# An expert-choice router on rows not yet normed: tile 6's and half of tile 7's routing inside the last output projection

## The chip, the cores and the metric

The kernel runs on one core of one Trainium2 chip. The metric is the device time of one execution in microseconds (us), as the median of several. The engines are TensorE (PE; its weight loads are PEld), VectorE (DVE), ScalarE (ACT), GpSimd (POOL) and SyncE (SP, which here only issues DMAs).

## The reference, cut to what matters

One layer over 1024 latent tokens of width 1024. Attention heads and mLSTM heads give `mix`; its output projection and the residual are normed; the normed rows are modulated and go to 16 experts, of which each picks its 128 best tokens by a softmax over experts.

```python
mix = jnp.concatenate([att, ml], axis=-1) @ w_out
x_new = _layer_norm(DEEPNORM_ALPHA * x + g1 * mix, ln1_g, ln1_b)
h = x_new * (1 + sc2) + sh2
aff = jax.nn.softmax(jnp.einsum('btd,de->bte', h, w_router), axis=-1)
g, idx = lax.top_k(jnp.swapaxes(aff, 1, 2), cap)          # cap = 128 tokens for each expert
y = ((jax.nn.silu(xe @ wg) * (xe @ wu)) @ wd) * g_e[..., None]   # for each expert, xe = h[idx_e]
x_new = _layer_norm(DEEPNORM_ALPHA * x_new + g2 * moe, ln2_g, ln2_b)
```

## The kernel before, in words

After the attention stage, `phase_tail` does the output projection in 8 tiles of 128 tokens, then the experts. Every float32 product is three products of rounded parts (high by high, high by low, low by high).

**The projection.** A tile has two halves of 512 columns; a half is 8 slices `k` by 3 products, 24 products into one PSUM bank (`mm_out`, L1405). `add_half` (L1412) adds the residual into `z` on DVE and takes statistics; `stats` (L1417, L1418) ends them, with the square root on ACT; `norm` (L1423 to L1429) writes the modulated normed row `h` on DVE and sends it to DRAM (`H2`); `normed` and two passes on POOL write the row that the experts' results are added to (`ACC`, L1435 to L1437). A tile's routing runs one tile later: while tile t is projected, tile t-1 is transposed from `h` (`transposed`, L1448) and multiplied by the router's weights (`router`, L1456, result `ps_lg`), then `soft_a` and `soft_b` (L1461 to L1473) make the affinities `AFF` and their bfloat16 parts `AUX`.

**The ranks of experts 0 and 1.** `row_of` (L1479) spreads the affinities of a tile along a row `R`; `rank_a` and `rank_own` (L1495, L1504, L1506) compare on DVE; `rank_b` (L1513, result `ps_k`) counts with one-column products. They run two tiles late. `slots` adds the counts, `slots_of` (L1822) makes one-hots `oh`, `index_of` (L1829 to L1842) turns them into token numbers `idx` and gathers those rows of `H2` into `xe` with an indirect DMA on POOL; `tokens_of` (L1853 to L1856) transposes them into `xeH` and `xeL`. The other experts' choices come later, from 16 rounds of a maximum on DVE (L1755, L1757) during expert 0.

**Weights.** SP streams expert weights in tiles of 1 MB (`we_st`) into staging buffers: six at first, two more once the projection's memory is free. ACT casts each (`conv_h`, L1360, `weH`) and DVE takes the rest (`conv_l`, L1368, `weL`). Their ring has six places: four from pool `mA`, opened when the projection's memory is closed, and two from pool `mB`, opened when the memory `ow` of the token tiles is closed. So the fifth and sixth weight tile go where token tiles were.

**Order.** Each engine runs its instructions in the order in which the code writes them (a manual schedule), and so does each DMA queue. After tile 7's last product come, before the change: tile 6's router, the rest of tile 7's norm, its transposes and router, the ranks of tiles 6 and 7 for expert 0, the index, the gather, and the first expert products `ps_gu` (L1619). Between them ACT and DVE take the first weight tiles.

Of the kernel before, what the change touches and what calls it, by code (L numbers as in the profile page):

```python
# [165 lines left out]
class K:  # L166
# [1149 lines left out]
    def phase_tail(self, nexp=NE, final=True):  # L1316
# [103 lines left out]
        def norm(t):  # L1420
            ts = slice(128 * t, 128 * t + 128)
# [3 lines left out]
            h = hT[t] = ow.tile([128, D], F32, name="h2")  # L1425
            for cs in (slice(0, 512), slice(512, D)) if t == 7 else (slice(0, D),):
                nc.vector.scalar_tensor_tensor(h[:, cs], z[t][:, cs], s[:, 12:13], G2[:, cs], op0=ALU.subtract,
                                               op1=ALU.mult)
                nc.vector.scalar_tensor_tensor(h[:, cs], h[:, cs], s[:, 14:15], B2[:, cs], op0=ALU.mult, op1=ALU.add)  # L1429
                if t == 7 and cs.start == 0:  # L1430
                    soft_b(6)
            (nc.scalar if t == 7 else nc.gpsimd).dma_start(self.H2[ts], h)
            if t < 7:
                normed(t)
                nc.gpsimd.tensor_mul(xs[t], xs[t], AG)  # L1435
                nc.gpsimd.tensor_add(xs[t], xs[t], AB)
                nc.gpsimd.dma_start(self.ACC[ts], xs[t])  # L1437
# [4 lines left out]
        def transposed(t, between=None):  # L1442
            h, hT[t] = hT[t], ow.tile([128, 8, 128], F32, name="hT", bufs=1)
            for i in range(2):
# [4 lines left out]
                nc.scalar.copy(hT[t][:, 4 * i:4 * i + 4, :], pt)  # L1449
                if i == 0 and between:  # L1450
                    between()

        def router(t):
            sm[t] = self.pY.tile([128, 512], F32, name="ps_lg", tag="y")
            for k in range(8):
                nc.tensor.matmul(sm[t][:, :NE], hT[t][:, k, :], wr[:, k, :], start=(k == 0), stop=(k == 7))  # L1456

        def soft_a(t):
            ps = sm[t]
            m = sm[t] = ow.tile([128, 4], F32, name="rm")  # L1460
            nc.vector.tensor_reduce(m[:, 0:1], ps[:, :NE], axis=AX.X, op=ALU.max)  # L1461
            nc.vector.tensor_scalar(m[:, 1:2], m[:, 0:1], -1.0, None, op0=ALU.mult)
            nc.scalar.activation(self.aff(t), ps[:, :NE], AF.Exp, bias=m[:, 1:2], accum_out=m[:, 2:3])
# [531 lines left out]
```

## Time and profile before

| | |
|---|---|
| median of 3 executions | 2335.6 us (2334.59 to 2339.47) |
| profiled execution: time, span | 2338.02 us, 2336.2 us |
| PE, DVE, ACT, POOL busy | 95%, 84%, 61%, 21% of the span |
| mean granted PE clock | 0.977 of 2.4 GHz |
| chain that ended last: PE, DVE, issue, DMA | 72%, 13%, 5%, 4% |
| projection of 8 tiles | 639.5 to 750.7 us |
| first expert product | 778.95 us |

The profile is of one execution, and times in it run from its span's start. Busy is the time in which an engine had work, idle time before an instruction is put down to what released it. A line number is that of the kernel before. "Granted clock" is the share of 2.4 GHz that PE was given: 1.00 is 2.4 GHz, 0.50 is 1.2 GHz.

### The profile page before, as it was taken

To read this page: it belongs to the slowest core of one execution; us is meant where nothing else is said; L and a number is where in the kernel's file an instruction comes from. 1 tells how busy PE (TensorE), PEld (TensorE's weight loads), DVE (VectorE), ACT (ScalarE), POOL (GpSimd) and SP (SyncE) were. 2 spreads that over 40 slices of the span, in tenths; PEclk is the share of its full clock that TensorE was granted. 3 is DMA by queue.
4 is the path that set the end of the run, shared out by engine and by line. 5 is a ranking of instruction groups with operands and counts; after the bars stand their busy time and mean duration, and the time that the engine had idled before them with its cause. 6 is when DMAs were issued, how large, how long until landed. Compare 5 with 4: busy or idle time off the path is not lost.

```text
span 2336.2 us, 33448 instructions
## 1 busy us (share of the span) xinstructions
PE 2222.8 (95%) x12590; PEld 1913.1 (82%) x12590; DVE 1957.3 (84%) x2399; ACT 1428.2 (61%) x1556; POOL 497.5 (21%) x538
## 2 busy tenths in 40 slices
PE   7988999899999798999999999999999999999995
PEld 6888888789987676888888888888888888888884
DVE  6875588768866898898998988989889889898898
ACT  2333433348844665677676777777767767777673
POOL 3545456315444101001000010010000100100014
PEclk9999999899999898999999999999999999999998
DMA  7686447489767798999999999999999999999994
GB/s 297 204 277 224 129 136 221 151 271 336 234 224 249 259 353 306 332 368 377 396 370 381 384 371 392 373 378 387 373 390 377 370 394 375 380 389 370 399 385 193
DMA packets 350306, 746.31 MB, mean 319 GB/s; under 512 B 16576, under 2 KB 98944, under 8 KB 348480
## 3 DMA queue, kind: packets, MB, share of 16 engines
q1 hardware_dynamic: 332208, 681.44, 79.7%
q0 software_dynamic: 17648, 61.68, 8.6%
q8 instruction: 99, 1.62, 0.3%
q10 hardware_dynamic: 288, 1.05, 0.1%
q14 instruction: 63, 0.52, 0.1%
HBM read 687.20 MB, written 64.24 MB: 322 GB/s over the span
## 4 chain that ended last, share of the span: by engine, by line
PE 72%; DVE 13%; issue 5%; DMA 4%; ACT 2%; POOL 2%; SPq 0%; POOLq 0%; ACTq 0%; DVEq 0%
PE ps_gu L1619 38%; PE ps_y L1648 18%; PE ps_o L1405 3%; DVE weL L1368 3%; PE ps_o L1142 2%; PE ps_in L438 2%; PE ps_hT L1634 1%; PE ps_l L1052 1%; PE ps_tl L1101 1%; PE ps_lg L1456 1%; DVE y L546 1%; DVE mCL L894 1%; DMA MIX<-ev 1%; POOL wL L398 1%; PE ps_xe L1853 1%
## 5 line engine op out<-in xcount | busy, mean ns | idle before, releaser
L1368 DVE TENSOR_TENSOR weL<-we_st,weH 128x2048 fp32r<-128x2048 f32 x528 | 1181.0, 2284 | 85.6 <-ACT weH L1360 85.4
L1360 ACT CAST weH<-we_st 128x2048 fp32r<-128x2048 f32 x528 | 981.0, 1911 | 46.3 <-PE ps_y L1648 38.4
L1619 PE MATMUL ps_gu<-weH,xeH 128*128 128x512 f32 (+1 forms) x1536 | 581.6, 379 | 0.0
L1619 PE MATMUL ps_gu<-weH,xeL 128*128 128x512 f32 (+1 forms) x1536 | 573.3, 373 | 0.0
L1619 PE MATMUL ps_gu<-weL,xeH 128*128 128x512 f32 (+1 forms) x1536 | 572.4, 373 | 0.0
L1619 PEld LDWEIGHTS ps_gu<-weH,xeL 128*128 128x128 f32 x1536 | 290.1, 189 | 51.9 <-DVE xeL L1856 0.3
L1619 PEld LDWEIGHTS ps_gu<-weL,xeH 128*128 128x128 f32 x1536 | 290.6, 189 | 49.0
L1619 PEld LDWEIGHTS ps_gu<-weH,xeH 128*128 128x128 f32 x1536 | 290.4, 189 | 48.6 <-ACT xeH L1855 0.2
L1637 ACT CAST hTH<-ps_hT 128x512 fp32r<-128x512 f32 x96 | 52.9, 551 | 390.7 <-PE ps_hT L1634 390.7
L1648 PE MATMUL ps_y<-weH,hTH 128*128 128x512 f32 x700 | 218.7, 394 | 3.9 <-ACT hTH L1637 3.9
L1648 PE MATMUL ps_y<-weL,hTH 128*128 128x512 f32 x700 | 216.7, 391 | 0.0
L1648 PE MATMUL ps_y<-weH,hTL 128*128 128x512 f32 x700 | 216.4, 390 | 0.0
L1838 POOL TENSOR_SCALAR idx<-ax 128x1 int32<-128x1 f32 x15 | 5.5, 365 | 792.7 <-ACT ax L1831 792.7
L1648 PEld LDWEIGHTS ps_y<-weH,hTH 128*128 128x128 f32 x700 | 131.1, 189 | 30.6 <-ACT hTH L1637 4.1
L1648 PEld LDWEIGHTS ps_y<-weL,hTH 128*128 128x128 f32 x700 | 132.1, 189 | 27.8
L1648 PEld LDWEIGHTS ps_y<-weH,hTL 128*128 128x128 f32 x700 | 131.9, 188 | 28.0 <-DVE hTL L1638 0.2
L1701 POOL DMA_INDIRECT ACC<-yo,idx x15 | 28.9, 1924 | 544.8 <-DVE yo L1663 544.8
L438 PE MATMUL ps_in<-wH,uH 128*128 128x256 f32 (+1 forms) x448 | 131.8, 294 | 9.9 <-DVE ev L485 4.6
L438 PE MATMUL ps_in<-wL,uH 128*128 128x256 f32 (+1 forms) x448 | 129.0, 288 | 0.0
L438 PE MATMUL ps_in<-wH,uL 128*128 128x256 f32 (+1 forms) x448 | 128.9, 288 | 0.0
L1638 DVE TENSOR_TENSOR hTL<-ps_hT,hTH 128x512 fp32r<-128x512 f32 x96 | 61.5, 640 | 65.9 <-ACT hTH L1637 65.9
L438 PEld LDWEIGHTS ps_in<-wH,uH 128*128 128x128 f32 x448 | 87.7, 196 | 12.0 <-DVE ev L485 5.3
(438 smaller groups left out, 3674.7 us busy)
## 6 DMA issues: line engine op xcount, KB each, us to landing
we_st<-in_wg SPq DMA_DIRECT2D x176, 1024.0 KB, 10.0
we_st<-in_wu SPq DMA_DIRECT2D x176, 1024.0 KB, 10.0
we_st<-in_wd SPq DMA_DIRECT2D x176, 1024.0 KB, 9.7
wr<-in_w_ada POOLq DMA_DIRECT2D x32, 512.0 KB, 5.1
ws<-in_w_in POOLq DMA_DIRECT2D x36, 256.0 KB, 4.5
abi<-in_bias SPq DMA_DIRECT2D x16, 480.0 KB, 9.2
wa<-in_w_ada SPq DMA_DIRECT2D x7, 1024.0 KB, 7.4
u<-in_xcT SPq DMA_DIRECT2D x8, 640.0 KB, 7.6
```

The source lines that it names most:

```text
L398: nc.gpsimd.tensor_sub(L[:, s, :w], t[:, :, :w], f32(H[:, s, :w]))
L438: nc.tensor.matmul(ps[:, :w], l, r, start=(k == 0 and i == 0), stop=(k == 7 and i == 2))
L546: nc.vector.scalar_tensor_tensor(y[:, o:o + w], x[:, i0 + j:i0 + j + w], cw[:, j:j + 1], y[:, o:o + w], op0=ALU.mult, op1=ALU.add)
L1142: nc.tensor.matmul(o[:, cb, :], vt[:k, half:half + 64], pp[:k, col, :], start=(i == 0), stop=(i == 14))
L1360: nc.scalar.copy(H, staged[pos[2]])
L1368: nc.vector.tensor_sub(L, staged.pop(pos[1]), f32(H))
L1405: nc.tensor.matmul(ps, a[:, k, :], b, start=(k == 4 and j == 0), stop=(k == 3 and j == 2))
L1619: nc.tensor.matmul(ps[:, :w], a[:, k, :], b[:, kk, :], start=(n == 0), stop=(n == 23))
L1637: nc.scalar.copy(hH[:, :n], pt[:, :n])
L1638: nc.vector.tensor_sub(hL[:, :n], pt[:, :n], f32(hH[:, :n]))
L1648: nc.tensor.matmul(py[j], a[:, k, :], b[:, k % 2, 512 * j:512 * j + 512], start=(s == 0 and k == 0 and m == 0), stop=(s == 5 and k == n - ...
L1701: nc.gpsimd.indirect_dma_start(out=self.ACC, in_=yo, in_offset=None, compute_op=ALU.add, out_offset=bass.IndirectOffsetOnAxis(ap=idx[:, :1 ...
```

## The change

The router's product is taken on `z`, the row before its norm. With G2 and B2 the columns' scale and shift, mean and root of a row as scalars, the logits are the product of `z` with G2-scaled router weights, times the row's inverse root, plus a 16-wide correction `lg` from two column sums `wsum`. `fold` makes the scaled weights `wgb` and the sums once, at tile 0; G2 and B2 get there by way of DRAM (`GB`, then `gb`: 128 x 16 pieces of one element), on POOL's queue at the end of the attention stage.

The loop ends at tile 6 and tile 7 is written out: tile 6's transposes, router and softmax, tile 5's ranks, tile 6's row for expert 0 and the first half of tile 7's transposes and router stand between tile 7's products. After them stand the second half, then tile 7's softmax ahead of the second step of its norm. Its `H2` write goes from ACT's queue to POOL's. The first weight cast moves behind tile 7's `normed`, the two passes that make its `ACC` row move from before the index to behind the first two weight subtractions, and that write from ACT's queue to POOL's, behind the gather. The index for expert 0 is reduced on DVE from PSUM instead of from ACT's copy (`AUX` holds 128 times the tile's number for it).

```diff
@@ mix_rows @@
+        self.gb = self.orow.tile([128, 2, 8], F32, name="gb")
+        for i, row in enumerate((self.G2, self.B2)):
+            nc.gpsimd.dma_start(self.GB[i:i + 1], row[0:1])
+        nc.gpsimd.dma_start(self.gb, self.GB.rearrange("i (k p) -> p i k", p=128))
...
+        def fold():
+            for i in range(2):
+                nc.vector.tensor_tensor(wgb[:, i], wr, self.gb[:, i, :, None].to_broadcast([128, 8, NE]), op=ALU.mult)
+            ps = self.pY.tile([128, 512], F32, name="ps_w", tag="y")
+            nc.tensor.matmul(ps[:, :256], self.ones, wgb.rearrange("p i k e -> p (i k e)"), start=True, stop=True)
+            for i in range(2):
+                nc.vector.tensor_reduce(wsum[:, i], ps[:, 128 * i:128 * i + 128].rearrange("p (k e) -> p e k", k=8),
+                                        axis=AX.X, op=ALU.add)
...
+            lg[t] = ow.tile([128, NE], F32, name="lg")
+            nc.vector.scalar_tensor_tensor(lg[t], wsum[:, 0], s[:, 15:16], wsum[:, 1], op0=ALU.mult, op1=ALU.add)
...
-                    nc.tensor.transpose(pt[:, k, :], h[:, 128 * kk:128 * kk + 128], self.ident)
+                    nc.tensor.transpose(pt[:, k, :], z[t][:, 128 * kk:128 * kk + 128], self.ident)
...
+            nc.vector.scalar_tensor_tensor(x, ps[:, :NE], st[t][:, 14:15], x, op0=ALU.mult, op1=ALU.add)
...
-        for t in range(8):
+        for t in range(7):
...
-        transposed(7, lambda: row_of(6, (0,)))
+        t = 7
+        ps = [self.pG.tile([128, 512], F32, name="ps_o", tag="g") for _ in range(2)]
+        for n, k in enumerate(korder):
+            mm_out(t, ps[0], k, 0)
+            if n == 1:
+                transposed(6)
+                row_of(5)
+            if n == 5:
+                router(6)
+        gs = [rank_a(5, 0)]
...
+        add_half(t, ps[0], 0)
+        soft_a(6)
+        nc.scalar.activation(tiny, self.eps, AF.Sqrt)
+        soft_b(6)
+        for n, k in enumerate(korder):
+            mm_out(t, ps[1], k, 1)
+            if n == 1:
+                rank_b(5, 0, gs[0])
+                rank_b(5, 1, gs[1])
+            if n == 3:
+                transposed(7, (0,))
+            if n == 5:
+                row_of(6, (0,))
+            if n == 6:
+                router(7, range(4))
...
         ge = rank_a(6, 0)
         rank_own(6, 0, ge)
-        router(7)
-        normed(7)
-        nc.vector.tensor_mul(xs[7], xs[7], AG)
+        add_half(t, ps[1], 1)
         rank_b(6, 0, ge)
-        soft_a(7)
+        transposed(7, (1,))
+        router(7, range(4, 8))
+        stats(t)
+        nc.scalar.activation(tiny, self.eps, AF.Exp)
+        centred(7)
+        root(7)
+        soft_max(7)
...
+        scaled(7, slice(0, 512))
         soft_b(7)
         row_of(7, (0,))
         ge = rank_a(7, 0)
+        scaled(7, slice(512, D))
+        nc.gpsimd.dma_start(self.H2[896:], hT[7])
         rank_own(7, 0, ge)
-        rank_b(7, 0, ge)
+        rank_b(7, 0, ge, True)
         slots(0)
-        conv_h(2)
+        normed(7)
+        conv_h(1)
         oh = self.slots_of(0)
-        nc.vector.tensor_add(xs[7], xs[7], AB)
-        nc.scalar.dma_start(self.ACC[896:], xs[7])
         ew.close()
...
         info = {0: self.index_of(0, oh, mx)}
+        conv_h(2)
         conv_l(2)
+        nc.vector.tensor_mul(xs[7], xs[7], AG)
+        nc.vector.tensor_add(xs[7], xs[7], AB)
+        nc.gpsimd.dma_start(self.ACC[896:], xs[7])
         conv_h(3)
```

The orders below are those of the built programs; line numbers of the changed kernel differ from those of the kernel before. On PE, inside tile 7, where `row_of` of tile 5 (`ps_r`) meets the products of the first half (`ps_o`), the kernel before has all 24 of them ahead of the transposes `ps_ht`:

```order
L1405 MATMUL ps_o<-oH,mxH 128x512
L1405 MATMUL ps_o<-oL,mxH 128x512
L1405 MATMUL ps_o<-oH,mxL 128x512
L1448 MATMUL ps_ht<-cst,h_9175 128x128 x8
L1479 MATMUL ps_r<-cst,AFF 128x128 x2
L1405 MATMUL ps_o<-oH,mxH 128x512
```

and the change has tile 5's router `ps_lg` and then six products ahead of them:

```order
L1480 MATMUL ps_lg<-wgb,hT 128x16 x8
L1412 MATMUL ps_o<-oH,mxH 128x512
L1412 MATMUL ps_o<-oL,mxH 128x512
L1412 MATMUL ps_o<-oH,mxL 128x512
L1412 MATMUL ps_o<-oH,mxH 128x512
L1412 MATMUL ps_o<-oL,mxH 128x512
L1412 MATMUL ps_o<-oH,mxL 128x512
L1473 MATMUL ps_ht<-cst,z 128x128 x8
L1508 MATMUL ps_r<-cst,AFF 128x128 x2
L1412 MATMUL ps_o<-oH,mxH 128x512
```

So the rows of tile 5's affinities moved from behind 24 products of tile 7 to behind six.

On PE again, behind tile 7's last product and the `ps_k` of one tile, before:

```order
L1456 MATMUL ps_lg<-wr,hT 128x16 x8
L1448 MATMUL ps_ht<-cst,h_9326 128x128 x4
L1479 MATMUL ps_r<-cst,AFF 128x128
L1448 MATMUL ps_ht<-cst,h_9326 128x128 x4
L1456 MATMUL ps_lg<-wr,hT 128x16 x8
```

and now:

```order
L1473 MATMUL ps_ht<-cst,z 128x128 x4
L1480 MATMUL ps_lg<-wgb,hT 128x16 x4
L1508 MATMUL ps_r<-cst,AFF 128x128
L1542 LDWEIGHTS ge
L1542 MATMUL ps_k<-one_8331,ge 128x1
```

One whole router and half of another, and half of the transposes, went from behind the last product to places ahead of it.

On ACT, around its copy `ax` of the index's product, `weH` being weight casts and `xeH` the cast of the gathered rows, before:

```order
L1482 COPY R_8321<-ps_r 128x128
L1514 ACTIVATE cnt<-ps_k 128x7
L1360 CAST weH<-we_st 128x2048
L1590 DMA ACC<-xt 128x1024
L1831 COPY ax<-ps_i 128x5
L1360 CAST weH<-we_st 128x2048
L1482 COPY R_8322<-ps_r 128x128 x2
L1360 CAST weH<-we_st 128x2048 x2
L1855 CAST xeH<-ps_xe 128x512 x2
L1360 CAST weH<-we_st 128x2048 x2
```

and now:

```order
L1645 ACTIVATE AFF,rm<-lg,rm 128x16
L1511 COPY R_8326<-ps_r 128x128
L1464 ACTIVATE xt<-z,lst 128x1024
L1365 CAST weH<-we_st 128x2048
L1902 COPY ax<-ps_i 128x5
L1365 CAST weH<-we_st 128x2048 x2
L1511 COPY R_8327<-ps_r 128x128 x2
L1365 CAST weH<-we_st 128x2048 x2
L1927 CAST xeH<-ps_xe 128x512 x2
L1365 CAST weH<-we_st 128x2048 x2
```

The DMA of `ACC` is gone from ACT; in both orders five casts stand ahead of `xeH`, and now all but the first of them stand behind `ax`.

On DVE in the same place (`xt` is tile 7's row for `ACC`), before:

```order
L1517 TENSOR_REDUCE SL<-cnt 128x8
L1822 TENSOR_SCALAR oh<-cst,SL 128x128 x8
L1589 TENSOR_TENSOR xt<-xt,AB 128x1024
L1836 SCALAR_TENSOR_TENSOR idx<-ax 128x1
L1368 TENSOR_TENSOR weL<-we_st,weH 128x2048 x4
L1856 TENSOR_TENSOR xeL<-ps_xe,xeH 128x512 x2
```

and now:

```order
L1549 TENSOR_REDUCE SL<-cnt 128x8
L1893 TENSOR_SCALAR oh<-cst,SL 128x128 x8
L1908 TENSOR_REDUCE idx<-ps_i 128x1
L1373 TENSOR_TENSOR weL<-we_st,weH 128x2048 x2
L1668 TENSOR_TENSOR xt<-xt,AG 128x1024
L1669 TENSOR_TENSOR xt<-xt,AB 128x1024
L1373 TENSOR_TENSOR weL<-we_st,weH 128x2048 x2
L1928 TENSOR_TENSOR xeL<-ps_xe,xeH 128x512 x2
```

The two passes over `xt`, one of which stood far ahead and one just before the index, now stand behind the index and two weight subtractions.

## Rows read from the trace of the kernel before

**Rows 1.** Stretches: length, busy us by engine (PE, PEld, DVE, ACT, POOL), PEclk, DMA.

```profile
738.00:739.00 1.00, 1.00 (x3) 0.78 (x3) 0.99 (x1) 0.99 (x4) 0.00 (x0) 0.50 1.02 391
...
751.00:779.00 28.00, 12.86 (x79) 10.29 (x76) 22.40 (x46) 15.64 (x24) 12.16 (x15) 0.57 0.53 206
...
797.00:910.00 113.00, 98.65 (x477) 81.41 (x475) 111.55 (x114) 73.92 (x55) 9.42 (x5) 0.95 0.92 331
...
1000.00:2300.00 1300.00, 1298.73 (x6327) 1090.42 (x6327) 1168.58 (x793) 926.20 (x665) 110.89 (x79) 1.00 1.03 380
```

**Rows 2.** Timeline, DVE: start, length, line, operation, out<-in, count, [idle before <-releaser].

```profile
793.80 2.29 DVE L1368 TENSOR_TENSOR weL<-we_st,weH 128x2048 fp32r<-128x2048 f32 x1 [4.62 <-ACT weH L1360]
```

**Rows 3.** Timeline of ACT around the first expert product.

```profile
770.59 3.72 ACT L1360 CAST weH<-we_st 128x2048 fp32r<-128x2048 f32 x2
...
778.31 0.59 ACT L1855 CAST xeH<-ps_xe 128x512 fp32r<-128x512 f32 x1 [4.00 <-PE ps_xe L1853]
...
791.77 0.18 ACT L1514 ACTIVATE cnt<-ps_k 128x6 f32<-128x6 f32 x1 [6.39 <-PE ps_k L1513]
```

**Rows 4.** Timeline of PE, tile 7 to the first expert product.

```profile
735.17 1.96 PE L1456 MATMUL ps_lg<-wr,hT 128*128 128x16 f32 x16 [0.17 <-ACT cnt L1514]
...
737.79 0.63 PE L1405 MATMUL ps_o<-oH,mxH 128*128 128x512 f32 x1
...
741.18 0.39 PE L1405 MATMUL ps_o<-oH,mxL 128*128 128x512 f32 x1
...
750.72 0.40 PE L1513 MATMUL ps_k<-one,ge 128*128 128x1 bf16 x10
...
778.95 0.79 PE L1619 MATMUL ps_gu<-weH,xeH 128*128 128x512 f32 x1
```

**Rows 5.** Timeline of DVE from tile 6's affinities to the index.

```profile
740.42 0.23 DVE L1468 TENSOR_SCALAR AFF<-AFF,rm 128x16 f32<-128x16 f32 x1
...
750.91 0.69 DVE L1412 SCALAR_TENSOR_TENSOR z<-xt,ps_o 128x512 f32<-128x512 f32 x1 [2.49 <-PE ps_o L1405]
...
760.08 1.23 DVE L1578 TENSOR_TENSOR xt<-xt,AG 128x1024 f32<-128x1024 f32 x1 [1.07 <-ACT xt L1440]
...
762.86 0.23 DVE L1468 TENSOR_SCALAR AFF<-AFF,rm 128x16 f32<-128x16 f32 x1
...
765.23 1.66 DVE L1822 TENSOR_SCALAR oh<-cst,SL 128x128 bf16<-128x128 f32 x8
...
768.62 0.16 DVE L1836 SCALAR_TENSOR_TENSOR idx<-ax 128x1 int32<-128x1 f32 x1 [0.60 <-ACT ax L1831]
```

**Rows 6.** Timeline of POOL, tile 6's row write and the first gather.

```profile
740.61 0.57 POOL L1432 DMA_DIRECT2D H<-h  x1 [6.65 <-DVE rm L1467]
...
769.06 2.83 POOL L1839 DMA_INDIRECT xe<-H,idx  x1 [4.39 <-DVE idx L1836]
```

**Rows 7.** Chain that ended last: start, length, what, count.

```profile
744.30 0.87 PE ps_ht L1448 x8
...
745.39 5.48 PE ps_o L1405 x24
```

**Rows 8.** DMA issues, 739-742 us, then 690-705: count, KB, us to landing.

```profile
H<-h POOLq DMA_DIRECT2D x1, 512.0 KB, 2.9
...
H<-h POOLq DMA_DIRECT2D x1, 512.0 KB, 8.7
...
ACC<-xt POOLq DMA_DIRECT2D x1, 512.0 KB, 5.0
```

**Rows 9.** Timeline of POOL at the end of the attention stage.

```profile
630.11 1.28 POOL L1167 TENSOR_TENSOR aoL<-aoz,aoH 64x512 fp32r<-64x512 f32 x1
...
636.36 1.28 POOL L1167 TENSOR_TENSOR aoL<-aoz,aoH 64x512 fp32r<-64x512 f32 x1 [3.92 <-ACT aoH L1166]
```

**Rows 10.** Timeline of SP's DMA queue before tile 0's first sum.

```profile
642.59 0.33 SPq L1400 DMA_DIRECT2D xt<-in_x  x1
```

**Rows 11.** Timeline of DVE, tile 0's first sum.

```profile
650.86 0.69 DVE L1412 SCALAR_TENSOR_TENSOR z<-xt,ps_o 128x512 f32<-128x512 f32 x1 [1.52 <-PE ps_o L1405]
```

More of the change, by code (lines that the diff above doesn't have):

```diff
@@ L211, in consts @@
         self.ACC = dr.tile([SEQ, D], F32, name="ACC")
+        self.GB = dr.tile([2, D], F32, name="GB")
         self.AFF = cp.tile([128, 4, 2, NE], F32, name="AFF")
@@ L1395, in phase_tail @@
         tiny = orow.tile([128, 1], F32, name="tiny")
-        xs, z, st, hT, sm = {}, {}, {}, {}, {}
+        wgb = orow.tile([128, 2, 8, NE], F32, name="wgb")
+        wsum = orow.tile([128, 2, NE], F32, name="wsum")
+        xs, z, st, hT, sm, zT, lg = {}, {}, {}, {}, {}, {}, {}
         def load_x(t):
@@ L1418, in stats, with centred, root @@
             nc.scalar.activation(s[:, 14:15], s[:, 13:14], AF.Sqrt, bias=self.eps)
-        def norm(t):
-            ts = slice(128 * t, 128 * t + 128)
+        def centred(t):
+            h = hT[t] = ow.tile([128, D], F32, name="h2")
+            nc.vector.scalar_tensor_tensor(h, z[t], st[t][:, 12:13], G2, op0=ALU.subtract, op1=ALU.mult)
+        def root(t):
             s = st[t]
@@ L1424, in norm, with scaled, transposed @@
             nc.vector.scalar_tensor_tensor(s[:, 15:16], s[:, 12:13], -1.0, s[:, 14:15], op0=ALU.mult, op1=ALU.mult)
[L1425 to L1437, printed above, removed]
+            lg[t] = ow.tile([128, NE], F32, name="lg")
+            nc.vector.scalar_tensor_tensor(lg[t], wsum[:, 0], s[:, 15:16], wsum[:, 1], op0=ALU.mult, op1=ALU.add)
+        def scaled(t, cs):
+            h = hT[t]
+            nc.vector.scalar_tensor_tensor(h[:, cs], h[:, cs], st[t][:, 14:15], B2[:, cs], op0=ALU.mult, op1=ALU.add)
+        def norm(t):
+            ts = slice(128 * t, 128 * t + 128)
+            root(t)
+            centred(t)
+            scaled(t, slice(0, D))
+            nc.gpsimd.dma_start(self.H2[ts], hT.pop(t))
+            normed(t)
+            nc.gpsimd.tensor_mul(xs[t], xs[t], AG)
+            nc.gpsimd.tensor_add(xs[t], xs[t], AB)
+            nc.gpsimd.dma_start(self.ACC[ts], xs[t])
         def normed(t):
             nc.scalar.activation(xs[t], z[t], AF.Identity, scale=st[t][:, 14:15], bias=st[t][:, 15:16])
-        def transposed(t, between=None):
-            h, hT[t] = hT[t], ow.tile([128, 8, 128], F32, name="hT", bufs=1)
-            for i in range(2):
+        def transposed(t, halves=(0, 1)):
+            if 0 in halves:
+                zT[t] = ow.tile([128, 8, 128], F32, name="hT", bufs=1)
+            for i in halves:
                 pt = self.pT.tile([128, 4, 128], F32, name="ps_ht", tag="t")
@@ L1447, in transposed, with router, soft_max @@
                     kk = 4 * i + k
-                    nc.tensor.transpose(pt[:, k, :], h[:, 128 * kk:128 * kk + 128], self.ident)
[L1449 to L1456, printed above, removed]
-        def soft_a(t):
[L1459 to L1463, printed above, removed]
+                    nc.tensor.transpose(pt[:, k, :], z[t][:, 128 * kk:128 * kk + 128], self.ident)
+                nc.scalar.copy(zT[t][:, 4 * i:4 * i + 4, :], pt)
+        def router(t, ks=range(8)):
+            if ks[0] == 0:
+                sm[t] = self.pY.tile([128, 512], F32, name="ps_lg", tag="y")
+            for k in ks:
+                nc.tensor.matmul(sm[t][:, :NE], zT[t][:, k, :], wgb[:, 0, k, :], start=(k == 0), stop=(k == 7))
+        def soft_max(t):
+            ps, x = sm[t], lg[t]
+            m = sm[t] = ow.tile([128, 4], F32, name="rm")
+            nc.vector.scalar_tensor_tensor(x, ps[:, :NE], st[t][:, 14:15], x, op0=ALU.mult, op1=ALU.add)
+            nc.vector.tensor_reduce(m[:, 0:1], x, axis=AX.X, op=ALU.max)
+            nc.vector.tensor_scalar(m[:, 1:2], m[:, 0:1], -1.0, None, op0=ALU.mult)
+        def soft_a(t):
+            soft_max(t)
+            m = sm[t]
+            nc.scalar.activation(self.aff(t), lg.pop(t), AF.Exp, bias=m[:, 1:2], accum_out=m[:, 2:3])
         def soft_b(t):
@@ L1535, in phase_tail @@
                         mm_out(0, ps[i], k, i)
+                fold()
                 add_half(0, ps[0], 0)
@@ L1565, in phase_tail @@
             norm(t)
-            if 0 < t < 7:
+            if t:
                 soft_b(t - 1)
```

34 lines of the change are left out of this document (21 added, 13 removed).

## The prediction

> **What bounds the kernel now.** I read the busy time by stretch first [rows 1]. From 1000 to 2300 us TensorE (PE) works 1298.73 of 1300 us at full clock: there the expert products alone set the pace, and whatever starts them earlier ends the kernel earlier. From 797 to 910 us VectorE (DVE) is the full engine, 111.55 of 113 us. In between lies the change's stage, 751 to 779 us, where PE is busy for less than half of the time at a mean granted clock of 0.57. Does a gain there get through the DVE stretch? The reader is to see that DVE stands idle for 4.62 us before that stretch, until 793.80, for a cast of ScalarE (ACT), and ACT itself had waited 6.39 us for narrow products that stand on PE behind the first 48 expert products [rows 2, 3]. So DVE's full stretch begins when PE lets it, and moves with the first expert product.
>
> So one length counts. Call P the start of the narrow products `ps_k` behind the last projection product, 750.72 us; the first expert product starts at 778.95, P+28.23 [rows 4]. On the way the chain of waits names DVE, ACT and PE in turn, each for tenths of a microsecond, then the gather of 128 token rows. The marks on it: tile 7's affinities `AFF` at P+12.14, one-hot `oh` at P+14.51, the index at P+17.90 [rows 5], the gather on GpSimd (POOL) at P+18.34 [rows 6], the cast `xeH` of its transposed rows at P+27.59 [rows 3].
>
> **Part 1: PE work moved ahead of P.** The products of one half of a tile are 24 in 5.48 us, 0.228 us each; eight transposes take 0.87, and a row of affinities as much as one of them, 0.11 [rows 7]. Router products of one tile keep PE for 1.8 us (1.96 by the row, less the overlap with the next) [rows 4]. Now ahead of P stand also tile 6's router (1.8; it lay behind P, beside DVE's statistics), tile 5's `ps_k` (0.40 by its row [rows 4], 0.5 with the gap behind it), half of tile 7's transposes (0.44), one affinity row (0.11) and half of its router (0.9): 3.75 us. The fold adds one 256-column product `ps_w`; no row shows it, a 512-column one takes 0.23 and a whole router 1.8, I take 0.4.
>
> Against this something new is late. The affinity rows of tile 5 now follow six products instead of 24. They need `AFF` of tile 5, which DVE writes at 740.42 [rows 5]; two new 16-wide operations, 0.2 us each like `AFF` itself (0.23), stand ahead, so 740.8, and PE can go on at about 741.3. PE would reach that place at 739.2 (735.17, the router's 1.8, six products, eight transposes) and so waits 2 us. In the execution before, PE ran eight products at half clock just there, 737.79 to 741.18, 0.42 us apart instead of 0.228, and lost 1.6 us [rows 4]; that loss now hides in the wait. From 741.3: 42 products (9.56) and the 3.75 give 754.6, with `ps_w` 755.0. P moves by **+4.3 us**. The execution profiled took 2338.0 us, 1.8 of it outside its span; the median of the runs shown, 2335.6, is 2.4 lower. If the median run lacked the slow stretch, its P would move by 1.6 more: a bound for the slow side.
>
> **Part 2: from P to the index.** What goes: normalising before the transposes, half of the transposes, the wait for both. New order on DVE: sum `z` at P+0.2, statistics, centring (1.3, a pass over 1024 columns as at 760.08 [rows 5]) to P+3.2, six dependent operations of 16 or fewer columns, 0.2 each, to P+4.4. Beside them PE transposes the second half (0.44), ACT copies it (0.6, the size of `xeH` [rows 3]) and PE multiplies (0.9), all done by P+3.1, and ACT takes the root and loads the exponential's table: hidden behind DVE's six operations. Then exponential, half of the scaling, reciprocal, `AFF` at P+5.2. From `AFF` to `oh` DVE took 2.37 [rows 5]; the other half of the scaling (0.7, the size of the sum at 750.91) now stands in between: `oh` at P+8.25, 1.66 for it, index at P+10.25 straight from PSUM, without ACT's copy. POOL starts its gather 0.44 after the index, as before [rows 5, 6]: P+10.7 instead of P+18.34, **7.6 us shorter**. The small operations added to tiles 0 to 6 (some 0.4 us a tile) lie in DVE's idle time before each sum, 2.49 us in the row of tile 7 [rows 5]; without that they would cost 3.
>
> The gather needs tile 7's rows in DRAM. Their write leaves ACT's queue for POOL's, behind five small casts, at P+7.3. On POOL such a write landed in 2.9 us with the transfers quiet and in 8.7 beside weight and mix loads [rows 8]. Quiet is nearest: the two weight loads started at P are through by then. It lands at P+10.2, just in time; at 8.7 the gather would start at P+16.0.
>
> **Part 3: from the gather to the products.** `xeH` came 9.25 us after the gather's start [rows 3, 6], which would now be P+20.0. But ACT works in order, and ahead of `xeH` stands the cast of the fifth weight tile, the second of the two at 770.59 [rows 3]. Its ring buffer lies where the tile-7 rows were, so it cannot begin before their last use: the write of `xt` to ACC. Before, ACT itself sent that write ahead of its copy for the index, early enough. Now it waits for two passes on DVE, which come after two weight subtractions (2.29 each [rows 2]): P+10.25 + 4.6 + 2 x 1.23 [rows 5] = P+17.3, and then for POOL, behind the gather (2.83 [rows 6]). From P+17.3 it lands in 2.9 to 8.7 us; I take 5.0, the `ACC` row beside weight and mix loads [rows 8], since weight loads run again by then. The cast ends at P+17.3 + 5.0 + 1.9 = P+24.2, and the first product follows `xeH` by 0.64 as before: P+24.8. Of the 7.6 us **3.4 are left**. What waits behind the cast: `xeH`, DVE's `xeL`, PE.
>
> **Part 4: before the tiles.** Three more DMAs stand on POOL behind the G2 product, the last of them 2048 pieces of 4 bytes, and it waits for the other two to land. The pending `aoL` at 630.11 [rows 9] is held for two issues, a landing (2.9) and a third issue. POOL then idles 3.92 before 636.36, and behind that the load of `xt` leaves at 642.59 [rows 10] and is wanted by the first sum at 650.86 [rows 11]; with 2.9 for 512 KB [rows 8] that leaves 5.4. A hold of up to 9.3 us is covered; I count nothing.
>
> **Sum:** +4.3 - 3.4 = +0.9, on 2335.6: **2336.5 us**, which is no change. About 0.2% (4.7 us) is what a measurement of this kernel can tell from no change.
>
> **Rivals.**
> A, the ACC write does not hold: it lands in 2.9 us. Then the cast ends at P+22.1, and the two further subtractions on DVE end at P+21.9, so `xeL` and the first products come at about P+22, 6.2 earlier than before: -1.9, 2333.7. If the products also meet a clock that rises sooner (before, the first one took 0.79, and eight products at half clock cost 1.6 [rows 4]), 2332. For it: the write to DRAM of 2.9; against it: weight loads beside it.
> B, the clock falls again in tile 7. PE's granted clock was 0.50 (1.2 GHz) around 738 us [rows 1] after router and `ps_k` products, narrow ones, and now tile 7 mixes more of those, a 2 us wait and transposes into its products. Eight products at half clock again: +1.6, 2338.1. The Trainium skill, "TensorE: Matmul & The Clock Gate", Part 4: PE-mode transpose, says that transposes do not count as busy for the clock; by that rule this rival would be the likely case, and the time 2338.1. The trace is no clear witness, since tiles 1 to 6 carry the same transposes and mostly kept full clock.
> C, slower: the 4-byte load holds POOL. Its issue is priced between that of a 128-row write, 0.57 [rows 6], and 16 times that for 16 times the pieces, 9.1. It decides from a hold of 9.3 us on: two issues 1.1 + landing 2.9 + 9.1 = 13.1 is 3.8 too long, with a landing of 8.7 it is 9.6. Then the `xt` load and the mix loads behind it are late and PE stands at tile 0 or 1: 2340.3 to 2346. Against it: a price for each piece shows in no row, and the write's 0.57 [rows 6] is the nearest.
> D, the writes land late, 8.7 instead of 5.0: the cast ends 3.7 later, 2340.2.
> E, the change does not do what it says: AFF of tile 7 is no earlier relative to P (a wait I miss). Then the shift stays and the gain goes: 2339 to 2341.
>
> **Chances.** Forecast 0.42, A 0.25, B 0.12, C 0.07, D 0.09, E 0.05. Faster by over 0.2% is only A with both its bonuses and an error in P's shift: 0.11. Slower by over 0.2%: C whole, half of D and E, and a sixth of forecast and B together with the median's missing slow stretch: 0.21. Same: 0.68. The range leaves out the upper half of C and the best of A: 2331.5 to 2341.5.
>
> **What would show it.** Right: PE waits about 2 us for `AFF` in tile 7 after six products; from the last projection product to the gather 10.7 us; ACT idle ahead of the fifth weight cast, released by the ACC write, with `xeH` behind it. Wrong: the gather later than P+12 (the row write), POOL's `aoL` after 640 us (C), products of tile 7 0.43 us apart (B), or an expert stretch whose length differs by more than 1 us.

## The result and the profile after

The change takes 2345.74 us (median of 6, 2342.59 to 2349.62); the kernel before 2335.1 (median of 6 in the same comparison). The ratio is 1.0057, with a 95% interval of 1.0046 to 1.0068: by the ratio about 13 us slower, by the medians 10.6. The prediction was 2336.5 in 2331.5 to 2341.5, no change.

The profiled execution took 2342.59 us, span 2340.8, clock 0.972. I cut the span at four marks and measure from the last transpose `ps_tc` of the attention stage, because what lies ahead of it scatters in every kernel (622 to 634 us in the fourteen traces of this study, the kernel before included). **Lead-in** goes from there to the first projection product, **projection** to P, **gap** to the first expert product, **experts** to the end of the span. Both kernels were profiled twice:

| stretch (us) | before | before, 2nd | change | change, 2nd | predicted shift |
|---|---|---|---|---|---|
| lead-in | 6.46 | 6.45 | 12.17 | 12.50 | 0 |
| projection | 111.17 | 111.13 | 120.65 | 119.52 | +4.3 |
| gap | 28.23 | 28.31 | 25.98 | 26.23 | -3.4 |
| experts | 1557.25 | 1556.49 | 1559.00 | 1559.87 | 0 |
| sum | 1703.11 | 1702.38 | 1717.80 | 1718.12 | +0.9 |

The gap is shorter by 2.2, as forecast in kind. Nearly all of the loss lies ahead of P, in two stretches of which I priced one at nothing and half of the other.

**Lead-in.** PE's timeline of the change, then of the kernel before, at the end of the attention stage:

```profile
623.00 0.38 PE L1104 MATMUL ps_tc<-cst,apt 128*128 128x128 f32 x2
624.14 0.41 PE L1133 MATMUL ps_o<-cst,am 128*64 128x128 f32 x2 [0.76 <-ACT ars L1154]
629.16 0.48 PE L1143 MATMUL ps_o<-aPH,avr 96*64 96x128 f32 x2 [4.61 <-DVE aoz L1155]
...
635.17 0.45 PE L1412 MATMUL ps_o<-oH,mxH 128*128 128x512 f32 x1
```

```profile
633.09 0.38 PE L1103 MATMUL ps_tc<-cst,apt 128*128 128x128 f32 x2
634.23 0.40 PE L1132 MATMUL ps_o<-cst,am 128*64 128x128 f32 x2 [0.76 <-ACT ars L1153]
635.67 0.33 PE L1142 MATMUL ps_o<-aPH,avr 96*64 96x128 f32 x2 [1.04 <-DVE aoz L1154]
...
639.55 0.44 PE L1405 MATMUL ps_o<-oH,mxH 128*128 128x512 f32 x1
```

PE waits 4.61 us for `aoz` where it waited 1.04, and then works at half clock (0.50 from 629.2 to 633.8): from the end of the wait to the first projection product it needs 6.01 us instead of 3.88. POOL's and DVE's timelines say why:

```profile
620.35 0.57 POOL L1275 DMA_DIRECT2D GB<-G  x1 [0.29 <-POOL G L1272]
620.91 0.50 POOL L1275 DMA_DIRECT2D GB<-B  x1
625.89 1.21 POOL L1276 DMA_DIRECT2D gb<-GB  x1 [4.48 <-issue]
627.11 1.27 POOL L1168 TENSOR_TENSOR aoL<-aoz,aoH 64x512 fp32r<-64x512 f32 x1
```

```profile
628.42 0.68 DVE L1155 TENSOR_TENSOR aoz<-ps_o,ars 64x512 f32<-64x512 f32 x1 [3.48 <-POOL aoL L1168]
```

`aoL` had its input `aoH` at 618.9 (ACT's cast, 618.26 and 0.61 long), but POOL stood for 4.48 us at the load of `gb`, which waits for the two rows to land in DRAM. The list of DMA issues of 620 to 627 us, the last column being the time to landing:

```profile
GB<-G POOLq DMA_DIRECT2D x1, 4.0 KB, 4.2
GB<-B POOLq DMA_DIRECT2D x1, 4.0 KB, 4.4
gb<-GB POOLq DMA_DIRECT2D x1, 8.0 KB, 3.9
```

The issue of the load itself took 1.21. In each of the six traces with the load at this place it starts 0.5 us behind the later of the two landings. So POOL was held for 6.8 us (620.35 to 627.11), and `aoL` began 8.2 us after its input instead of 1.1; and `aoz`, which has one buffer (bufs=1), can't be written by DVE before `aoL` has read it.

**Projection.** PE waits there three times:

```profile
674.78 0.50 PE L1412 MATMUL ps_o<-oH,mxH 128*128 128x512 f32 x1 [0.24 <-DMA mxH<-MIX]
...
677.07 0.50 PE L1412 MATMUL ps_o<-oH,mxL 128*128 128x512 f32 x1 [1.56 <-DMA mxL<-MIX]
...
742.00 0.40 PE L1508 MATMUL ps_r<-cst,AFF 128*128 128x128 f32 x2 [1.84 <-DVE AFF L1497]
```

The last is the wait for `AFF` of tile 5 that I forecast as 2 us. The first two are for tile 3's mix loads. Followed back through DVE, POOL and SP:

```profile
647.15 0.49 DVE L1429 TENSOR_REDUCE wsum<-ps_w 128x16 f32<-128x128 f32 x2 [2.15 <-PE ps_w L1427]
647.56 0.68 DVE L1419 SCALAR_TENSOR_TENSOR z<-xt,ps_o 128x512 f32<-128x512 f32 x1
```

```profile
660.14 0.58 POOL L1461 DMA_DIRECT2D ACC<-xt  x1 [0.30 <-POOL xt L1460]
```

```profile
663.15 0.34 SPq L1407 DMA_DIRECT2D xt<-in_x  x1
...
664.08 0.45 SPq L1306 DMA_DIRECT2D mxH<-MIX  x1
664.62 1.73 SPq L1306 DMA_DIRECT2D mxL<-MIX  x1
```

The two sums of `fold` (`wsum`) stand ahead of tile 0's first sum `z` on DVE and wait for `ps_w`, which stands behind tile 0's 48 products on PE. So tile 0's statistics, its `ACC` write and the load of `xt` into the same buffer come later, and the mix loads are queued behind that `xt` on SP. They landed 10.7 and 12.4 us after their issue.

And products ran at half clock, 0.43 us apart instead of 0.228: in the first trace 8 in tile 4 and 8 in tile 6 (tiles are counted from 0), in the second 13 in tile 3 and 3 in tile 7, there among narrow products that ran at half clock too. The kernel before has 8 in each trace, once in tile 7 [rows 4] and once in tile 5. Eight such products cost 1.6 us. Stretches of the change, columns as in [rows 1]:

```profile
629.20:633.80 4.60, 4.60 (x41) 4.56 (x42) 3.98 (x5) 3.23 (x4) 2.56 (x4) 0.50 0.43 95
691.00:692.00 1.00, 1.00 (x6) 0.87 (x6) 0.68 (x5) 1.00 (x1) 0.00 (x0) 1.00 0.00 0
...
693.00:694.00 1.00, 1.00 (x4) 0.81 (x3) 0.96 (x2) 0.80 (x1) 0.00 (x0) 0.50 0.88 344
694.00:695.00 1.00, 1.00 (x3) 0.75 (x3) 0.97 (x2) 0.00 (x0) 0.00 (x0) 0.50 1.03 393
```

The first row is the end of the attention stage, the others lie in tile 4.

What the moved work costs shows in tile 7 where no product of it runs at half clock. From its first product to P, in the second trace of the kernel before and then in the first of the change, columns as above:

```profile
731.76:743.90 12.14, 12.14 (x61) 9.96 (x60) 8.15 (x22) 5.56 (x10) 6.48 (x7) 1.00 0.40 154
```

```profile
737.64:755.82 18.18, 16.20 (x99) 13.31 (x99) 13.21 (x35) 6.84 (x16) 8.40 (x14) 1.00 0.28 107
```

PE is busy for 4.1 us more, at a granted clock of 1.00 in both; nearly all of the rest is the wait for `AFF`.

**Gap.** The rows that answer to [rows 3 to 6], DVE, POOL, ACT and PE:

```profile
761.03 0.23 DVE L1497 TENSOR_SCALAR AFF<-AFF,rm 128x16 f32<-128x16 f32 x1
...
764.06 1.66 DVE L1893 TENSOR_SCALAR oh<-cst,SL 128x128 bf16<-128x128 f32 x8
766.20 0.16 DVE L1908 TENSOR_REDUCE idx<-ps_i 128x1 int32<-128x2 f32 x1 [0.48 <-ACT ax L1902]
```

```profile
763.42 0.57 POOL L1651 DMA_DIRECT2D H<-h  x1 [0.18 <-issue]
767.21 2.27 POOL L1911 DMA_INDIRECT xe<-H,idx  x1 [3.22 <-DMA H<-h]
...
773.45 0.61 POOL L1670 DMA_DIRECT2D ACC<-xt  x1 [1.50 <-DVE xt L1669]
```

```profile
779.36 1.90 ACT L1365 CAST weH<-we_st 128x2048 fp32r<-128x2048 f32 x1 [7.47 <-DMA ACC<-xt]
781.17 1.07 ACT L1927 CAST xeH<-ps_xe 128x512 fp32r<-128x512 f32 x2
```

```profile
755.82 0.30 PE L1542 MATMUL ps_k<-one,ge 128*128 128x1 bf16 x6
...
774.77 1.97 PE L1925 MATMUL ps_xe<-cst,xe 128*128 128x128 f32 x8 [8.28 <-DMA xe<-H,idx]
781.80 0.79 PE L1690 MATMUL ps_gu<-weH,xeH 128*128 128x512 f32 x1 [5.06 <-ACT xeH L1927]
```

From P = 755.82: `AFF` at P+5.21, `oh` at P+8.24, the index at P+10.38, the gather at P+11.39, by the profile released by the landing of tile 7's rows; the `ACC` write at P+17.63; the fifth weight cast waits 7.47 us for it, `xeH` comes behind that, and PE, which transposes the gathered rows from P+18.95, starts the products at P+25.98.

### The profile page after: what moved, and what is told of

Same layout as the page of the kernel before. It is cut to its first block, busy times and chain, and to the rows that moved or that the text cites. A ratio compares the mean times of both kernels' runs of the same rounds, so it can differ in the third digit from the quotient of the medians.

```text
span 2340.8 us, 33484 instructions
## 1 busy us (share of the span) xinstructions
PE 2227.3 (95%) x12592; PEld 1918.2 (82%) x12592; DVE 1962.5 (84%) x2419; ACT 1428.8 (61%) x1556; POOL 504.5 (22%) x543
## 4 chain that ended last, share of the span: by engine, by line
PE 57%; DVE 6%; issue 2%; DMA 1%; ACT 1%; POOL 1%; POOLq 0%; DVEq 0%; ACTq 0%
PE ps_gu L1690 37%; PE ps_y L1719 18%; DVE weL L1373 3%; PE ps_hT L1705 1%; PE ps_xe L1925 1%; ACT weH L1365 0%; DMA zt<-ACC 0%; DVE m L1826 0%; DVE R L1828 0%; DVE zt L2013 0%; DVE hh L1698 0%; PE ps_i L1900 0%; DVE zeros L1987 0%; POOL zeros L1994 0%; POOL zeros L2004 0%
```

## The experiments

Two theories stood against each other from here: that the loss is made of these waits and each can be taken away alone, or that something else holds each place and the wait only shows it. The stretches of all runs, by the marks above:

| run | median us (n) | ratio to before, 95% | lead-in | projection | gap | experts | sum |
|---|---|---|---|---|---|---|---|
| e1_gb_late | 2343.77 (4) | 1.0053 (1.0034 to 1.0072) | 6.45 | 123.71 | 26.06 | 1557.85 | 1714.07 |
| e3_xe_first | 2340.51 (7) | 1.0032 (1.0019 to 1.0046) | 12.33 | 121.38 | 20.77 | 1559.25 | 1713.73 |
| e4_rows_late | 2345.32 (1) | | 12.31 | 119.59 | 26.15 | 1558.59 | 1716.64 |
| e5_all | 2332.59 (11) | 0.9992 (0.9978 to 1.0006) | 6.44 | 119.41 | 21.08 | 1557.79 | 1704.72 |
| e6_best | 2332.79 (12) | 1.0003 (0.9992 to 1.0013) | 6.44 | 117.55 | 20.68 | 1559.25 | 1703.92 |
| e7_gb_aux | 2342.90 (8) | 1.0045 (1.0032 to 1.0058) | 6.45 | 123.62 | 26.12 | 1558.04 | 1714.23 |
| e8_before_hold | 2343.42 (6) | 1.0043 (1.0030 to 1.0057) | 10.63 | 112.80 | 28.17 | 1558.91 | 1710.51 |
| e9_fold_late | 2350.63 (1) | | 12.46 | 118.61 | 26.15 | 1560.92 | 1718.14 |
| e10_lean | 2328.02 (6) | 0.9971 (0.9959 to 0.9983) | 7.97 | 115.79 | 20.28 | 1559.99 | 1704.03 |
| e10_again | 2332.20 (12) | 0.9993 (0.9982 to 1.0005) | 6.46 | 113.90 | 20.28 | 1558.09 | 1698.73 |

**e1_gb_late: the hold.**

```diff
@@ mix_rows @@
-        nc.gpsimd.dma_start(self.gb, self.GB.rearrange("i (k p) -> p i k", p=128))
@@ phase_tail @@
+        nc.gpsimd.dma_start(self.gb, self.GB.rearrange("i (k p) -> p i k", p=128))
         nc.gpsimd.memset(cnt, 0.0)
```

> Edit: only the 4-byte load of gb moves, from between POOL's mix_rows and the next aoL to behind the last aoL. Theory (hold): POOL's aoL waited for this load, DVE's one aoz buffer waited for aoL, and PE for aoz. Then from the last attention transpose ps_tc to the first product ps_o, 6.46 us before and 12.17 in the change, it takes about 7.5 (before's 6.46 and 1.1 for the two row writes that stay), and the kernel gains 4 to 5 us on the change, to about 2341. Rival (other cause: the weight halves oH and oL are what is late there): the stretch stays at 11 us or more, the wait for aoz at 4 us, and the time at 2345.7.

The lead-in is back at 6.45, so the wait for `aoz` was the hold. A gain in time is not shown (1.0053 against 1.0057, the intervals overlap): the projection grew by 3.1. The moved load now holds POOL's memset of `cnt`, DVE's first write of `cnt` waits for that, and the low weight half `oL` behind it on DVE is late. DVE's and PE's timelines of this run:

```profile
641.63 0.36 DVE L1557 TENSOR_SCALAR cnt<-cst 128x8 f32<-128x8 f32 x2 [2.24 <-POOL cnt L1394]
```

```profile
643.17 0.61 PE L1412 MATMUL ps_o<-oL,mxH 128*128 128x512 f32 x1 [2.15 <-DVE oL L1314]
```

Eight products at half clock follow that wait. It is the fault of the change in kind, made again a few instructions later, but not a landing this time: the two rows had landed 9 us before, and POOL lost 1.0 us ahead of the load and 1.2 in issuing it.

**e7_gb_aux: the load behind memset and the AUX passes.**

```diff
         nc.gpsimd.tensor_copy(self.AUX[:, :, :, 1], ...)
+        nc.gpsimd.dma_start(self.gb, self.GB.rearrange("i (k p) -> p i k", p=128))
```

> Edit: only the load of gb moves, now behind the last aoL, the memset of cnt and the two AUX passes. Theory (hold): the stretch ahead of the first projection product falls from 12.17 to 6.45 as before, and this time no new wait for oL follows (at most 0.6, the kernel before had 0.52): 5.7 less than the change, about 2340. Rival (with the hold gone the projection meets weights not yet split, whatever POOL does): the wait for oL stays at 2 us, and the time at 2343.

No wait for `oL` any more, and the time is still 2342.9. `gb` lands later, PE waits 0.99 for `wgb`, tile 0's statistics are later again, and the wait for the mix loads grows to 2.31, with eleven half-clock products behind it:

```profile
676.08 0.80 PE L1411 MATMUL ps_o<-oH,mxL 128*128 128x512 f32 x1 [2.31 <-DMA mxL<-MIX]
```

Neither theory as written: the lead-in gives back 5.7 and the projection takes 3.0 of it (1.0 for `wgb`, 0.8 more for the mix loads, the rest at half clock), because the next late thing stood 40 us behind. The time came out as the rival had it.

**e8_before_hold: the hold by itself**, the three DMAs in the kernel before.

```diff
@@ DRAM tensors of the kernel before @@
+        self.GB = dr.tile([2, D], F32, name="GB")
@@ mix_rows of the kernel before @@
+        self.gb = self.orow.tile([128, 2, 8], F32, name="gb")
+        for i, row in enumerate((self.G2, self.B2)):
+            nc.gpsimd.dma_start(self.GB[i:i + 1], row[0:1])
+        nc.gpsimd.dma_start(self.gb, self.GB.rearrange("i (k p) -> p i k", p=128))
```

> The kernel before, with only the three DMAs of G2 and B2 to DRAM and back to gb added on POOL, at the change's place; gb is not used. Theory (hold): it costs by itself what it costs in the change: from the last attention transpose to the first projection product 12.2 us instead of 6.46, PE's wait for aoz 4.5 instead of 1.04, about 2340 against 2334.4. Rival (the hold costs only together with the change's later steps): the stretch stays below 8 us and the time within 2 us of the kernel before.

```profile
635.86 0.47 PE L1143 MATMUL ps_o<-aPH,avr 96*64 96x128 f32 x2 [3.82 <-DVE aoz L1155]
```

PE's wait is 3.82 instead of 1.04 and the lead-in 4.2 longer. By its time the run is 10 us slower (7 to 13), which is most of what the whole change costs. The trace shows 7.4 of that: 4.2 in the lead-in, 1.6 in the projection, where the clock fell in two tiles instead of one, and 1.7 in the expert stretch; where the remaining 2.6 lie is not shown, and that the hold brought about the 1.6 and the 1.7 is not shown either. So three DMAs of 16 KB in all, on POOL at the wrong place, are enough to lose most of what the change loses.

**e9_fold_late: the mix loads.**

```diff
@@ fold @@
             nc.tensor.matmul(ps[:, :256], self.ones, ...)
+            return ps
+
+        def fold_sum(ps):
             for i in range(2):
                 nc.vector.tensor_reduce(wsum[:, i], ...)
@@ loop over tiles @@
-                fold()
+                pw = fold()
...
             stats(t)
+            if t == 0:
+                fold_sum(pw)
```

> Edit: only the two sums of fold in tile 0 move, from ahead of the first sum z to behind tile 0's statistics. Theory: DVE's first sum no longer waits for ps_w behind tile 0's 48 products; so tile 0's ACC write, the load of tile 2's xt on SP, which waits for it, and the mix loads of tile 3 queued behind that come 1.3 us earlier, and PE's wait for mxL at tile 3, 1.56 (0.96 in two other runs), falls below 0.3. Rival (the mix loads are late because the weight load ahead of them in the queue takes the bandwidth): the wait stays at 0.9 or more.

The wait for `mxL` is gone. It is in each of the six traces with the sums in their old place (0.96 to 2.31 us: both of the change, e1, e3, e4, e7), and in none of the five with the sums moved. So it was the order on DVE, through POOL and SP. The projection is 2.0 shorter than in the change's first trace, with as many products at half clock. Its single time, 2350.63, is no verdict: its experts took 1560.9 and its early part 630.7.

**e4_rows_late: the wait for AFF.**

```diff
             if n == 1:
                 transposed(6)
-                row_of(5)
             if n == 5:
+                row_of(5)
                 router(6)
```

> Edit: only tile 5's affinity rows move in tile 7, from behind 6 products to behind 18. Theory: PE's wait of 1.84 us for AFF goes, and the stretch from the first projection product to P falls from 120.65 to about 118.8. Rival: the wait reappears where PE needs the next thing from DVE (ps_k of tile 5, whose ranks start later), and the stretch stays at 120 or more.

The 1.84 is gone, and 0.84 comes back where the second group of `ps_k` wants a PSUM buffer that DVE has yet to read (`lg`). What the edit is worth alone this trace doesn't tell: tile 7 takes 18.4 us, in the change 18.2, because part of it runs at half clock here, and the projection, 119.59, is as long as in the change's second trace. In e5, which has the same edit and full clock in tile 7, that tile takes 17.1, 1.1 less than in the change.

**e3_xe_first: ACT's order in the gap.**

```diff
         conv_to(4)
-        conv_h(5)
         X = {0: self.tokens_of(info[0][2], mx)}
```

> Edit: only the cast of the fifth weight tile moves, from ahead of xeH to behind it on ACT. Theory (ACT's order): xeH stood 5 us behind a cast that waited for the ACC write. Then the first expert product comes about P+20.7 instead of P+25.98 (P is the ps_k behind the last projection product), and as PE no longer idles between ps_xe and the products, fewer of them run at half clock, worth another 1.3: about 2339.3. Rival (DVE sets the pace behind it): the first product comes as early, but the rest to the end of the span grows from 1559.0 by as much, time about 2345. Second rival: the products then wait for xeL or a weight tile, first product not before P+24.

ACT's and PE's timelines of this run, P = 767.68:

```profile
787.81 0.59 ACT L1926 CAST xeH<-ps_xe 128x512 fp32r<-128x512 f32 x1 [4.06 <-PE ps_xe L1924]
788.62 0.59 ACT L1926 CAST xeH<-ps_xe 128x512 fp32r<-128x512 f32 x1 [0.22 <-PE ps_xe L1924]
```

```profile
786.61 1.97 PE L1924 MATMUL ps_xe<-cst,xe 128*128 128x128 f32 x8 [8.27 <-DMA xe<-H,idx]
788.45 0.79 PE L1689 MATMUL ps_gu<-weH,xeH 128*128 128x512 f32 x1
```

The first product comes at P+20.77 instead of P+25.98, and the experts take no longer than in the change (1559.25 against 1559.00 and 1559.87), so the gain reaches the end: the median is 5.2 lower, the ratio 1.0032 instead of 1.0057. The cast that waited for the `ACC` write was what held `xeH`, and DVE's full stretch does not eat the gain.

**e5_all, e6_best: the parts together.** e5 joins e1, e3, e4 and e9; e6 puts the `gb` load where e7 has it and tile 5's two `ps_k` behind 12 products of the second half:

```diff
-            if n == 1:
+            if n == 3:
                 rank_b(5, 0, gs[0])
                 rank_b(5, 1, gs[1])
-            if n == 3:
                 transposed(7, (0,))
```

> Edit: the three edits of the other runs together, and in tile 0 the two sums of fold stand behind the statistics instead of ahead of the first sum z. Theory: the parts add up: 4.7 from the hold, 6.6 from ACT's order and the clock, 1.8 from the affinity rows and 1.3 because tile 0's ACC write, tile 2's xt load and tile 3's mix loads behind it come earlier (PE waited 1.8 for those): 14.4 less than the change, about 2331.3, that is 0.998 of the kernel before. Rival (DVE sets the pace in the expert stage, or the mix loads stay late): 2336 to 2338, no better than before.

> Edit: as the run with all parts, but the load of gb stands behind POOL's memset of cnt and its two AUX passes (so that DVE's write of cnt does not wait for it), and the two ps_k of tile 5 stand behind 12 products of tile 7's second half instead of 6. Theory: the 2.17 us wait for oL with the eight half-clock products behind it (1.6) and the 1.11 us wait for lg go; the stretch from the first projection product to P falls from 119.4 to about 115, the rest stays (6.45 ahead, 21.0 behind P, 1558 for the experts). From the last attention transpose to the end that is 1700.5 against 1703.1 before: about 2330, ratio to the kernel before 0.998. Rival (each wait removed is followed by another half-clock stretch or by the next wait): the stretch stays at 118 or more and the time at 2332.6.

Together they take back the 13 us: both are level with the kernel before, and the gain of 0.2% that both theories had is not shown. e6 has no wait in the projection but 1.06 for `wgb`, and yet it takes 117.55 where I forecast 115: products ran at half clock in tiles 4 and 7, which the rival had. The work moved ahead of P costs 4.1 and buys 7.6 in the gap; more than the difference goes to that wait, to the second stretch at half clock, and to the experts, which take 2.0 longer than in the first trace of the kernel before.

**e10_lean, e10_again: less moved.** Tile 7's first half goes back behind P, and `ps_w` between tile 1's halves:

```diff
@@ loop over tiles @@
                 transposed(t - 1)
+                if t == 1:
+                    fold()
+                    shift(0)
...
             norm(t)
+            if t == 0:
+                fold_mul()
@@ tile 7 @@
-                transposed(7, (0,))
...
-            if n == 6:
-                router(7, range(4))
...
+        transposed(7, (0,))
         rank_b(6, 0, ge)
         transposed(7, (1,))
-        router(7, range(4, 8))
+        router(7)
```

> Edit: as the run with all parts and both later corrections, and besides: the product ps_w stands between tile 1's halves instead of behind tile 0 (its two products on DVE behind tile 0's norm), and the transposes and router products of tile 7's first half stand behind the last projection product again. Theory: PE no longer waits 1.06 us for wgb, and 1.45 us of PE work goes back to a place where PE waits for DVE anyway: to P 115 instead of 117.6, to the first expert product 21.0 instead of 20.7, in all 2.2 less than that run, about 2330, level with or 0.1% faster than the kernel before. Rival (PE is what is waited for behind P): the stretch to the first expert product grows by 1.4 or more and nothing is gained but the 1.06.

> The lean version once more, unchanged, for a second trace and a second interval, because its first trace (1704.0 us from the last attention transpose to the end, against 1703.1 and 1702.4 of the kernel before) does not show the 0.29% by which its times were lower. Theory (the first trace was a slow one: 1.5 us of half-clock work ahead of the projection, 15 half-clock products in it, 13 behind it): now 1700 to 1702, and the ratio to the kernel before again 0.997 to 0.998. Rival (the first interval was luck of the early part, which scatters by 12 us): 1703 to 1704 again, and a ratio within 0.1% of 1.

The gap did not grow (20.28): the router products behind P are free, as PE waits for DVE there (the four transposes run just ahead of P). The first comparison gave 0.9971 and the second 0.9993, so the version is faster than the change, and faster than the kernel before by something between nothing and 0.4%. Its second trace, 1698.7, has one stretch at half clock in the projection, as the kernel before has, in tile 7:

```profile
737.50:740.00 2.50, 2.50 (x11) 2.20 (x11) 2.46 (x3) 1.93 (x5) 0.00 (x0) 0.50 0.99 379
```

Its first, with two such stretches and a lead-in partly at half clock, is level with the kernel before. Of the last expectation, the trace came out better than the theory (1700 to 1702) and the ratio as the rival had it, within 0.1% of 1.

**before_again, after_again** (unchanged kernels, for the scatter):

> The kernel before, unchanged, profiled once more. Theory: the stretches counted from the last attention transpose are steady and what scatters lies ahead of it (622 to 634 us in the ten traces so far): 6.5 to the first projection product, 111 to P, 28.2 to the first expert product, 1557 to the end, each within 1 us but for one stretch of half-clock products more or less (1.6). Rival: these stretches scatter as much as the early part, and differences of 2 us between traces say nothing.

> The change, unchanged, profiled once more. Theory: 12.2 to the first projection product, 120.7 to P with 1.5 us lost on mix loads and 1.84 on AFF, 26.0 to the first expert product, 1559 to the end, each within 1 us but for one stretch of half-clock products more or less (1.6). Rival: the waits of the first trace do not come back, and the loss lies elsewhere.

The table at the top has them. The kernel before repeats within 0.8 in each stretch. The change repeats its long lead-in and its wait for the mix loads (0.97, followed by 13 half-clock products). The wait for `AFF` is 0.24 in the second trace: PE comes to that place later, by products and transposes at half clock just ahead of it, and tile 7 is as long as in the first (18.19 and 18.18). Second trace:

```profile
740.00:742.00 2.00, 2.00 (x8) 1.60 (x8) 1.96 (x3) 1.41 (x3) 0.00 (x0) 0.50 1.03 391
```

```profile
743.07 0.40 PE L1508 MATMUL ps_r<-cst,AFF 128*128 128x128 f32 x2 [0.24 <-DVE AFF L1497]
```

## Why the prediction was wrong

**Part 4 failed**, the step "A hold of up to 9.3 us is covered; I count nothing". The hold was 6.8 us, under my bound, and cost 5.7 in the lead-in; by e8 it costs most of the loss by itself. I had asked how long POOL may be late for tile 0's loads, not who waits for the `aoL` that stands behind the DMAs: DVE's next `aoz`, by its one buffer, and through that PE. Rival C had the hold and the sign, but not the place (it has PE standing at tile 0 or 1), and its price (2048 pieces) and its threshold were wrong: the issue took 1.21, and the wait was for the two rows to land, 4.48 where I took 2.9. That the measured time lies within its bounds is luck. The Trainium skill, "DMA: Bandwidth & Descriptors", Anatomy of one DMA, fits a transfer on POOL's queue with 2.0 us plus a term for the bytes; for 4 KB that makes an estimate of 2.0. Here the rows landed in 4.2 and 4.4 beside the mix loads (3.3 to 4.5 in the twelve traces that have them), and the measurement decides.

**Part 1, "+4.3", measured +9.5 and +8.4.** The wait for `AFF` of tile 5 was forecast as 2 and was 1.84 ([rows 5] begins with tile 5's affinities, not with tile 6's as its heading says). The work moved into tile 7 was 3.75 by my sum and is 4.1 by PE's busy time. About that difference is lost where PE comes back from narrow products: the first wide one is followed after 0.31 to 0.32 us instead of 0.228, and tile 7 has five such places more. The sentence "that loss now hides in the wait" failed in the first trace: the slow stretch did not belong to that place. The kernel before has one in each trace, at another tile each time, the change two. In the second trace one of the two does hide in the wait for `AFF`, 0.24 there. Rival B had the price (1.6) right and named tile 7, where the first trace shows none and the second three products, at no cost. Whether transposes bring it about, as that rival considers, the runs don't tell: tiles with the same transposes ran both ways. And the 1.8 for the mix loads stood in no step: I called `fold` a product of 0.4 us and did not follow its two sums on DVE, which wait for that product ahead of `z`.

**Part 2 held.** `AFF` at P+5.2 (forecast P+5.2), `oh` at P+8.24 (P+8.25), index P+10.38 (P+10.25). The gather came at P+11.4, not 10.7. Tile 7's rows landed 3.0 after their issue at P+7.6, and so in the same moment in which the index was done (766.38 and 766.35); which of the two held the gather no run tells apart.

**Part 3 was right in kind, off by 1.2.** ACT idles ahead of the fifth cast, released by the `ACC` write, with `xeH` behind it; e3 shows that this is what held the products. The write left at P+17.6 (P+17.3) and took 5.7 (5.0). "Of the 7.6 us 3.4 are left" became 2.2.

**The experts** took 1.75 and 3.4 longer, of which the 13 and 8 half-clock products at their start (7 and 4 before) explain about 1. In every trace the granted clock is 0.50 when the products begin and rises 1.2 to 6.7 us later. What sets that, and the rest, stays open: the two traces of e10, one program with the same waits there, had 13 and 2 such products.

**The chances.** By the terms that the prediction gives, "slower" adds up to 0.23 (0.07, 0.07 and 0.09), not 0.21, and "same" to 0.66.

## What to carry to other kernels

A DMA that waits for another DMA, put on an in-order compute queue, holds every later instruction of that engine for a full landing; before counting it as covered, name the next instruction there, the buffer that it frees, how many such buffers there are, and who writes them. A reduction that is put ahead of the first operation of a pipeline inherits the wait for its input: what reads a product that stands behind a whole tile belongs behind that tile's statistics. And take several delays away together before judging: here a single repair gave 5 us at most, as the next wait took its place, and all of them gave 13.

## What the runs showed of the hardware that was not expected

Rows of 4 KB to DRAM took longer to land (4.2 and 4.4 us, beside loads) than the quickest writes of 512 KB in the same trace (2.9 and 3.0; others took up to 9.1), and a load of 2048 pieces of 4 bytes was issued by POOL in 1.21 us and landed in 3.9 (5.8 to 6.8 in the runs that issue it later). TensorE's clock fell to 0.50 for 7 to 13 products at a time, 0.43 us apart instead of 0.228, or for fewer where narrow products fell into the same stretch. Sometimes that came with a wait (behind e1's 2.15 us, in e7's 2.31), sometimes amid products that had followed each other without a gap (692 us in the change; the last idle time of PE before it was 0.25 us, at 689). None of the fourteen traces ran the projection without it; it came one to three times in each.
